# Attention sums and conformer taps on VectorE alone, and the conformer's place in w_o's order of K

## The chip, the cores and the metric

The kernel runs on one core of one Trainium2 chip. Its metric is the time of the device from start to end, in microseconds (us), the median of several executions. The core has five engines with a queue of instructions each: TensorE (PE; its weight loads are shown as PEld), VectorE (DVE), ScalarE (ACT), GpSimd (POOL) and SyncE (SP), which here only issues DMAs. An engine takes the instructions of its queue in order and waits on semaphores for what another engine or a DMA has to finish. TensorE reads its operands from SBUF and writes to PSUM.

## The reference

The reference computes two layers of a hybrid backbone over 128 context tokens and 1024 latent tokens of width 1024. In each layer three groups of heads work side by side on the projection of the normed input, and their outputs are joined and projected by `w_o`:

```python
attn_out = _blocked_attention(q, keys, vals)
conv_out = _conformer_conv(zc, p)
hy_out = _hyena(zh, p)
mix = jnp.concatenate([attn_out, conv_out, hy_out], axis=-1) @ p['w_o']
x = x + g1 * mix
```

Attention is softmax(q k / 8) v for 8 heads of 64, with 2 heads of keys and values, over 1152 keys for the latent tokens. The conformer gates its 256 channels, convolves each with 31 taps over the positions, norms them by groups and multiplies them by a 256 x 256 matrix. A convolutional feed-forward of width 2816 with a gate follows each layer. All is computed in float32; products that need it are split into a high and a low part, three matmuls in place of one.

## The kernel before

The planner that orders the queues takes the instructions of the program with a priority each, the place at which the program issued them; `high_priority(offset)` moves a stretch of them by so many places forward, a negative offset moves them back. Each engine's queue is then fixed.

A layer runs in four phases. Phase 1 norms the input, projects it and runs Hyena. Phase 2 (`phase2`) is attention, with the prompt's own attention, the conformer (`tapped_conv`) and parts of the modulation (`mod`) as generators in the background. Phase 3 (`phase3`) is the product with `w_o`, phase 4 the feed-forward.

In `attention`, j runs over 4 pairs of heads, half over 2 halves of 512 queries, c over 9 chunks of 128 keys: 72 chunks a layer. For a chunk TensorE makes the scores S^T of two heads in one PSUM tile (`st`, 128 x 1024, one buffer), ScalarE their exponentials `p` (128 x 1024 in SBUF, five buffers), and TensorE multiplies these by the values (`av`) two chunks later (`drain(2)`). The maxima that softmax needs are found ahead: `maxes(j + 1)` runs beside pair j, three products `S` and three reductions `mx` on VectorE a step, and its result goes into the score product as two more rows of q. The denominators are sums over the keys. `gather` first adds the exponentials of several chunks into a tile `es` of 128 x 1024; `finish` then multiplies each such tile by ones (`avs`, L1440) and divides. Of the nine chunks of a half, 0 and 1 are held and become the first terms of two sums; the even chunks are added on GpSimd (four adds), the odd ones on VectorE (three adds). Only in the last half of the layer does chunk 8 go into the ones product as a third part of its own, and there the reciprocals are spread by TensorE (`rs`, `orr`) and not by DMA.

`taps` convolves two blocks of 128 channels by 31 taps, with even and odd positions kept apart so that three sets of 16, 15 and 16 taps over 584 positions do it. Each tap is one VectorE instruction (L227, `ca<-cu,cws,ca`, `ca<-cd,cwh,ca`, `ca<-cu,cwh,ca`), 300 places back (`TAPS_PRIO`). Ten of the last 16 are done elsewhere: ScalarE multiplies (`cz<-cu,cwh`), GpSimd adds them up (`cz<-cz`), and one VectorE add joins them. After each VectorE tap the generator yields; `tapped_conv` hands control back every sixth time (`P2_TAPS`), and attention turns each background generator once a chunk, three times from chunk 41 on. When the taps are through, `conv` does the conformer's norms and its product, and `mix_out` writes its two blocks of output (chunks 4 and 5 of the 1024 rows of K in `w_o`) to DRAM as high and low part.

`phase3` loads the eight chunks of K, high (`mh`) and low (`ml`), each into a pool of its own; chunks 0 to 3 are attention's pairs, 4 and 5 the conformer's, 6 and 7 Hyena's. The loads are issued on SP in the order in which `w_o`'s product takes them (`MIX`), and the pools are opened in nearly the same order. The rows of `w_o` are put in that order on the host.

Of the kernel before, what the change touches and what calls it, by code (L numbers as in the profile page):

```python
# [31 lines left out]
RESIDUES = [0, 4, 2, 6, 1, 5, 3, 7]  # L32
PAIRS = [(0, 4), (2, 6), (1, 3), (5, 7)]

MIX = [6, 7, 4, 5, 0, 1, 2, 3]

# [80 lines left out]
SEGF = [(0, 386, 0, 386), (386, 770, 386, 770), (770, 1154, 770, 1152)]  # L119


P2_TAPS, TAPS_PRIO = 6, 300

SIDE_TAPS = 10

OUT_PRIO = 100

# [9 lines left out]
class Kern:  # L137
# [1236 lines left out]

    def attention(self, l, bgs):
        nc, ap, K1, K2, V = self.nc, self.ap, self.K1, self.K2, self.V
        pend, acc, fins, part, held = [], {}, [], [], {}

        def gather(j, half, c, P):

            k = c % 2
            if c < 2:
                held[k] = P
            elif j == 3 and half == 1 and c == 8:
                part.append(P)
            else:
                if c < 4:
                    part.append(ap.tile([128, 1024], F32, tag=f"e{k}", name="es", bufs=1))
                self.add(part[k][:], held[k][:] if c < 4 else part[k][:], P[:], None if k else nc.gpsimd)

        def drain(n):
            while len(pend) > n:
                j, half, c, P = pend.pop(0)
                g = j // 2
                if c == 0:
                    acc[0] = [self.sq.tile([128, 512], F32, tag=f"av{u}", name=n) for u, n in enumerate(("av", "avs"))]
                o, sm = acc[0]
                for u in range(2):
                    self.mm(o[64 * u : 64 * u + 64, :], V[:, 2 * c + g, :], P[:, 512 * u : 512 * u + 512], c == 0, c == 8)
                if c == 8:  # L1400
                    fins.append(self.finish(l, j, half, acc[0], list(part), j == 3 and half == 1))
                    part.clear()

        Q = self.first
        for j in range(4):
            g = j // 2
            cur, mg, nxt = Q, self.maxes(j + 1) if j < 3 else iter(()), None
            for half in range(2):
                for c in range(9):
                    S = self.sq.tile([128, 2, 512], F32, tag="st", name="st")  # L1410
                    for k, (K, n) in enumerate(((K1[g], 128), (K2[g], 66))):
                        for u in range(2):
                            self.mm(S[:, u, :], K[:n, 128 * c : 128 * c + 128], cur[u][k][:n, 512 * half : 512 * half + 512], k == 0, k == 1)
                    P = ap.tile([128, 1024], F32, tag="p", name="p", bufs=5)
                    self.act(P[:], S[:].rearrange("p a b -> p (a b)"), AF.Exp)
                    nxt = next(mg, nxt)
                    pend.append((j, half, c, P))
                    gather(j, half, c, P)
                    drain(2)
                    for f in fins:  # L1420
                        next(f, None)
                    for b in bgs:
                        for _ in range(3 if 9 * half + c + 18 * j > 40 else 1):
                            next(b, None)
            Q = nxt
            for Q in mg:
                pass
        drain(0)
        for f in fins:
            for _ in f:  # L1430
                pass
# [35 lines left out]
    def taps(self, l, tp):  # L1467


        nc, v, w = self.nc, self.vec[l], self.cwh[l]  # L1470

        n = 584
        for c in range(2):
            U = tp.tile([128, 1198], F32, tag="cu", name="cu", bufs=1)
            for p, q in ((0, 15), (143, 158), (1182, 1198)):
                nc.gpsimd.memset(U[:, p:q], 0.0)
            nc.sync.dma_start(U[:, 15:143], self.uD[c, :, 0:128])
            nc.sync.dma_start(U[:, 158:1182], self.uD[c, :, 128:NT])
            e, d = U[:].rearrange("p (m u) -> p u m", u=2)[:, 0, :], U[:].rearrange("p (m u) -> p u m", u=2)[:, 1, :]
            D = tp.tile([128, 598], F32, tag="cd2", name="cd2", bufs=1)  # L1480
            O = tp.tile([128, 1168], F32, tag="ca", name="ca", bufs=1)
            y0, y1 = O[:].rearrange("p (m u) -> p u m", u=2)[:, 0, :], O[:].rearrange("p (m u) -> p u m", u=2)[:, 1, :]
            h = w[:, 31 * c : 31 * c + 31]

            def low():
                return self.tc.high_priority(offset=-TAPS_PRIO)

            with low():
                self.sub(D[:], e[:, 1:599], d[:, 0:598])
                self.sub(e[:, 0:599], e[:, 0:599], d[:, 0:599])  # L1490
            yield

            Z = None
            for k in range(16 - SIDE_TAPS, 16):
                y = tp.tile([128, n], F32, tag="cz" if Z is None else "cy", name="cz", bufs=1 if Z is None else 2)
                self.act(y[:], e[:, k : k + n], AF.Copy, scale=h[:, 2 * k : 2 * k + 1])
                if Z is None:
                    Z = y
                else:
                    self.add(Z[:], Z[:], y[:], nc.gpsimd)  # L1500
            for k in range(16):
                with low():
                    s = h[:, 30:31] if k == 15 else self.cws[l][:, 15 * c + k : 15 * c + k + 1]
                    if k == 0:
                        nc.vector.tensor_scalar(y0, d[:, 0:n], s, v[:, V_CB + c : V_CB + c + 1], op0=ALU.mult, op1=ALU.add)
                    else:
                        self.stt(y0, d[:, k : k + n], s, y0, ALU.mult, ALU.add)
                yield
            for k in range(15):
                with low():  # L1510
                    self.stt(y1, D[:, k : k + n], h[:, 2 * k + 1 : 2 * k + 2], y1 if k else y0, ALU.mult, ALU.add)
                yield
            for k in range(16 - SIDE_TAPS):
                with low():
                    self.stt(y0, e[:, k : k + n], h[:, 2 * k : 2 * k + 1], y0, ALU.mult, ALU.add)
                yield
            if Z is not None:
                self.add(y0, y0, Z[:])
            nc.sync.dma_start(self.cD[c, :, 0:128], O[:, 0:128])
            nc.sync.dma_start(self.cD[c, :, 128:NT], O[:, 143:1167])  # L1520
        yield
# [56 lines left out]
    def phase3(self, l, bgf):  # L1578
# [5 lines left out]
        with ExitStack() as ctx:  # L1584
            self.use(self.ring(ctx, f"o{l}", 3, 5))
            src = self.i["xT"] if l == 0 else self.xD
            mh, ml = {}, {}
            for c in (3, 6, 7, 4, 5, 0, 1, 2):
                mp = self.pool(ctx, f"mix{l}{c}", 1, "right")
                mh[c], ml[c] = (mp.tile([128, NT], F32R, tag=t, name=t) for t in ("mh", "ml"))  # L1590
            for n, c in enumerate((6, 7, 4, 5, 0, 1, 2, 3)):
                nc.sync.dma_start(mh[c][:].bitcast(F32), self.mixD[l][0, c])
                nc.sync.dma_start(ml[c][:].bitcast(F32), self.mixD[l][1, c])
            for c in range(8):
# [289 lines left out]
```

## Time and profile before

| what | value |
|---|---|
| median of 3 runs | 3346.62 us (3346.41 to 3347.53) |
| the profiled execution's own time | 3345.59 us |
| its span, first to last instruction | 3343.3 us |
| mean granted clock of TensorE | 0.958 |
| TensorE busy | 3134.0 us, 94% |
| VectorE busy | 2160.7 us, 65% |
| ScalarE busy | 1195.1 us, 36% |
| GpSimd busy | 495.1 us, 15% |

Busy is the time in which an engine had at least one instruction running. The clock is the share of TensorE's full speed that was granted. Line numbers such as L227 are those of the kernel; many operations go through helpers and so share a line, and are told apart by their tiles, written out<-in. "pd", "up", "dn" and "wo" are phases 3 and 4, where TensorE is nearly always busy.

### The profile page before, as it was taken

Reading aid. Unit: us, or ns where it says so; the run is one execution under the profiler, and the core shown is the slowest. Engines: PE = TensorE matmul, PEld = TensorE weight load, DVE = VectorE, ACT = ScalarE, POOL = GpSimd, SP = SyncE. Lnnn points to the kernel's source line nnn. Section 1 sums busy time; section 2 is a strip of 40 time slices with the busy share of each in tenths; the row PEclk is TensorE's granted clock in tenths of the full one; section 3 lists DMA queues with packets and bytes.
Section 4 is the critical chain, followed back from the end, with each engine's and each line's share of the span. In section 5 each row is a group of like instructions: output and inputs, shape, how many; then the busy total and the mean of one; then the engine's idle time right before and its main releaser. Section 6 shows DMA issues by size and latency. Waiting matters only on the chain. (4 is left out here: it accounts for less than half of the span.)

```text
span 3343.3 us, 44669 instructions
## 1 busy us (share of the span) xinstructions
PE 3134.0 (94%) x17330; PEld 2769.0 (83%) x17330; DVE 2160.7 (65%) x3464; ACT 1195.1 (36%) x1976; POOL 495.1 (15%) x412
## 2 busy tenths in 40 slices
PE   5899778999799999999998997899999999999997
PEld 3899733449799999999998995345799999999997
DVE  6887889665765554545567896987365454554556
ACT  3433333452352222333344333435343233333223
POOL 5402234221310000000012113422110000000002
PEclk8899879999899999999999997899999999999998
DMA  7565544445311111111113446351511111111112
GB/s 280 172 224 173 158 151 168 156 161 163 127 38 42 42 44 43 42 42 44 42 56 134 161 142 212 100 164 61 190 29 51 42 42 43 43 42 42 42 44 70
DMA packets 152327, 336.08 MB, mean 101 GB/s; under 512 B 21360, under 2 KB 57844, under 8 KB 145589
## 3 DMA queue, kind: packets, MB, share of 16 engines
q1 hardware_dynamic: 147412, 318.69, 29.8%
q0 software_dynamic: 4704, 14.55, 1.5%
q8 instruction: 137, 2.24, 0.3%
q14 instruction: 74, 0.60, 0.1%
HBM read 264.86 MB, written 68.31 MB: 100 GB/s over the span
## 5 line engine op out<-in xcount | busy, mean ns | idle before, releaser
L241 PE MATMUL up<-hl,whi 128*128 128x384 f32 (+1 forms) x2112 | 712.8, 338 | 4.4 <-DVE hl L227 2.9
L241 PE MATMUL up<-hh,whi 128*128 128x384 f32 (+1 forms) x2112 | 710.3, 338 | 3.6 <-ACT hh L212 2.7
L241 PE MATMUL up<-hh,wlo 128*128 128x384 f32 (+1 forms) x2112 | 711.9, 337 | 0.0
L215 DVE TENSOR_TENSOR wlo<-wraw,whi 128x512 fp32r<-128x512 f32 x362 | 255.6, 706 | 646.6 <-ACT whi L235 646.3
L235 ACT CAST whi<-wraw 128x512 fp32r<-128x512 f32 x362 | 223.7, 618 | 848.2 <-PE dn L241 358.1
L241 PEld LDWEIGHTS up<-hl,whi 128*128 128x128 f32 x2112 | 398.7, 189 | 6.4 <-DVE hl L227 4.3
L241 PEld LDWEIGHTS up<-hh,whi 128*128 128x128 f32 x2112 | 398.7, 189 | 4.3 <-ACT hh L212 3.1
L241 PEld LDWEIGHTS up<-hh,wlo 128*128 128x128 f32 x2112 | 398.8, 189 | 0.0
L227 DVE SCALAR_TENSOR_TENSOR xt<-dn,mod,xt 128x128 f32<-128x128 f32 (+2 forms) x704 | 332.5, 514 | 71.3 <-PE dn L241 71.1
L241 PE MATMUL dn<-gh,wlo 128*128 128x384 f32 (+1 forms) x1056 | 359.0, 340 | 0.0
L241 PE MATMUL dn<-gh,whi 128*128 128x384 f32 (+1 forms) x1056 | 358.1, 339 | 0.0
L241 PE MATMUL dn<-gl,whi 128*128 128x384 f32 (+1 forms) x1056 | 357.4, 338 | 0.0
L227 DVE SCALAR_TENSOR_TENSOR fu<-pd,vec,fu 128x1154 f32<-128x1154 f32 (+2 forms) x192 | 254.0, 1324 | 91.7 <-ACT fu L212 89.2
L215 POOL TENSOR_TENSOR acc<-acc,sq 128x384 f32<-128x384 f32 x51 | 55.0, 1087 | 1633.2 <-ACT sq L212 1632.2
L241 PE MATMUL win<-hl,whi 128*128 128x384 f32 x768 | 265.0, 345 | 9.5 <-DVE hl L227 5.5
L241 PE MATMUL win<-hh,whi 128*128 128x384 f32 x768 | 264.0, 347 | 3.4 <-ACT hh L235 1.1
L241 PE MATMUL win<-hh,wlo 128*128 128x384 f32 x768 | 263.8, 344 | 0.0
L1357 DVE TENSOR_REDUCE mx<-S 128x1 f32<-128x384 f32 x384 | 196.6, 548 | 37.4 <-PE S L241 36.5
L1678 ACT COPY pd<-up 128x384 f32<-128x384 f32 (+1 forms) x352 | 131.8, 401 | 239.1 <-PE up L241 239.1
L212 ACT ACTIVATE p<-st 128x1024 f32<-128x1024 f32 x144 | 147.1, 1022 | 158.3 <-PE st L241 157.9
L241 PEld LDWEIGHTS dn<-gl,whi 128*128 128x128 f32 x1056 | 199.9, 189 | 0.0
L241 PEld LDWEIGHTS dn<-gh,whi 128*128 128x128 f32 x1056 | 199.7, 189 | 0.0
(294 smaller groups left out, 5196.7 us busy)
## 6 DMA issues: line engine op xcount, KB each, us to landing
wmod<-in_w_mod SPq DMA_DIRECT2D x48, 1024.0 KB
wraw<-in_w_up SPq DMA_DIRECT2D x176, 256.0 KB
wraw<-in_w_dn SPq DMA_DIRECT2D x88, 256.0 KB
wraw<-in_w_in SPq DMA_DIRECT2D x64, 256.0 KB
q<-qD SPq DMA_DIRECT2D x48, 256.0 KB
mh<-mixD SPq DMA_DIRECT2D x16, 576.0 KB
ml<-mixD SPq DMA_DIRECT2D x16, 576.0 KB
khD<-fK SPq DMA_DIRECT2D x16, 512.0 KB
```

The costliest lines, as they stand in the source:

```text
L212: return self.nc.scalar.activation(out, in_, f, **k)
L215: return (eng or self.nc.vector).tensor_tensor(out, a, b, op=op)
L227: return (eng or self.nc.vector).scalar_tensor_tensor(out, a, s, b, op0=op0, op1=op1)
L235: self.nc.scalar.copy(hi, src)
L241: self.nc.tensor.matmul(out, l, r, start=start, stop=stop)
L1357: nc.vector.tensor_reduce(m3[:, k, s : s + 1], S[:, :384], op=ALU.max, axis=AX.X)
L1678: self.nc.scalar.copy(p[:, u + o : v + o], t[:, u - a : v - a])
```

## The change

Four edits. In `gather` the exponentials of chunks 0 to 7 are added up in one tile `e` with two buffers, seven adds on VectorE, and chunk 8 goes into the ones product as the second part, in every half. In `taps` the side sum on ScalarE and GpSimd is gone and all 47 taps a block run on VectorE; control goes back every eighth tap, and the taps stand 200 places back. The conformer's chunks 4 and 5 move in `MIX` from third and fourth to sixth and seventh, just ahead of chunk 3; the loads and the pools follow.

```diff
-MIX = [6, 7, 4, 5, 0, 1, 2, 3]
+MIX = [6, 7, 0, 1, 2, 4, 5, 3]
...
-P2_TAPS, TAPS_PRIO = 6, 300
-
-SIDE_TAPS = 10
+P2_TAPS, TAPS_PRIO = 8, 200
...
-        pend, acc, fins, part, held = [], {}, [], [], {}
+        pend, acc, fins, parts, held = [], {}, [], [], {}
...
-            k = c % 2
-            if c < 2:
-                held[k] = P
-            elif j == 3 and half == 1 and c == 8:
+            if c == 0:
+                held[0] = P
+                parts.append([])
+                return
+            part = parts[-1]
+            if c == 8:
                 part.append(P)
             else:
-                if c < 4:
-                    part.append(ap.tile([128, 1024], F32, tag=f"e{k}", name="es", bufs=1))
-                self.add(part[k][:], held[k][:] if c < 4 else part[k][:], P[:], None if k else nc.gpsimd)
+                if c == 1:
+                    part.append(ap.tile([128, 1024], F32, tag="e", name="es", bufs=2))
+                self.add(part[0][:], held[0][:] if c < 2 else part[0][:], P[:])
...
-                    fins.append(self.finish(l, j, half, acc[0], list(part), j == 3 and half == 1))
-                    part.clear()
+                    fins.append(self.finish(l, j, half, acc[0], parts.pop(0), j == 3 and half == 1))
...
-            Z = None
-            for k in range(16 - SIDE_TAPS, 16):
-                y = tp.tile([128, n], F32, tag="cz" if Z is None else "cy", name="cz", bufs=1 if Z is None else 2)
-                self.act(y[:], e[:, k : k + n], AF.Copy, scale=h[:, 2 * k : 2 * k + 1])
-                if Z is None:
-                    Z = y
-                else:
-                    self.add(Z[:], Z[:], y[:], nc.gpsimd)
...
-            for k in range(16 - SIDE_TAPS):
+            for k in range(16):
                 with low():
                     self.stt(y0, e[:, k : k + n], h[:, 2 * k : 2 * k + 1], y0, ALU.mult, ALU.add)
                 yield
-            if Z is not None:
-                self.add(y0, y0, Z[:])
...
-            for c in (3, 6, 7, 4, 5, 0, 1, 2):
+            for c in (3, 6, 7, 0, 1, 2, 4, 5):
...
-            for n, c in enumerate((6, 7, 4, 5, 0, 1, 2, 3)):
+            for n, c in enumerate(MIX):
```

## Rows read from the trace of the kernel before

**Rows 1.** The chain that ended last, layer 1: start us, us, what.

```profile
2179.94 2.71 DVE ml L215
...
2183.85 0.74 DVE ca L227
...
2186.39 1.13 DVE es L215
...
2189.35 2.23 DVE ca L227
```

**Rows 2.** From:to, us, PE PEld DVE ACT POOL busy (instructions), clock, DMA share, GB/s.

```profile
434.00:590.00 156.00, 130.26 (x527) 58.12 (x529) 148.06 (x234) 60.48 (x86) 66.11 (x34) 0.84 0.40 142
590.00:720.00 130.00, 124.75 (x632) 64.26 (x632) 91.08 (x179) 63.66 (x88) 34.77 (x15) 0.99 0.41 137
2073.00:2230.00 157.00, 132.39 (x550) 59.48 (x551) 155.65 (x236) 63.62 (x90) 66.07 (x35) 0.90 0.41 140
2230.00:2345.00 115.00, 111.06 (x540) 59.04 (x538) 86.50 (x168) 60.59 (x86) 31.25 (x13) 1.00 0.30 90
```

**Rows 3.** The same stretches, instructions that touch tile p alone; ACT counts exponentials.

```profile
434.00:590.00 156.00, 35.15 (x118) 6.32 (x120) 14.13 (x9) 30.67 (x30) 33.50 (x13) 0.84 0.40 142
590.00:720.00 130.00, 35.57 (x132) 6.41 (x132) 14.65 (x12) 33.03 (x33) 34.77 (x15) 0.99 0.41 137
2073.00:2230.00 157.00, 37.35 (x130) 6.77 (x132) 12.15 (x10) 33.77 (x34) 34.88 (x14) 0.90 0.41 140
2230.00:2345.00 115.00, 31.65 (x120) 5.87 (x118) 13.39 (x11) 30.03 (x30) 31.25 (x13) 1.00 0.30 90
```

**Rows 4.** VectorE's groups, 434 to 590 us: xcount | busy us, mean ns.

```profile
L1357 DVE TENSOR_REDUCE mx<-S 128x1 f32<-128x384 f32 x85 | 43.6, 547 | 4.5 <-PE S L241 4.4
L227 DVE SCALAR_TENSOR_TENSOR ca<-cu,cws,ca 128x584 f32<-128x584 f32 x28 | 33.3, 1189 | 0.1
L227 DVE SCALAR_TENSOR_TENSOR ca<-cd,cwh,ca 128x584 f32<-128x584 f32 x30 | 25.7, 855 | 0.0
L227 DVE SCALAR_TENSOR_TENSOR ca<-cu,cwh,ca 128x584 f32<-128x584 f32 x14 | 20.3, 1447 | 0.0
L215 DVE TENSOR_TENSOR es<-es,p 128x1024 f32<-128x1024 f32 x6 | 9.3, 1548 | 0.0
L215 DVE TENSOR_TENSOR es<-p 128x1024 f32<-128x1024 f32 x3 | 4.8, 1614 | 0.0
...
L215 DVE TENSOR_TENSOR cu<-cu 128x599 f32<-128x599 f32 x2 | 1.6, 776 | 0.0
```

**Rows 5.** VectorE's groups, 2073 to 2230 us.

```profile
L227 DVE SCALAR_TENSOR_TENSOR ca<-cu,cws,ca 128x584 f32<-128x584 f32 x28 | 37.9, 1354 | 0.1
L227 DVE SCALAR_TENSOR_TENSOR ca<-cd,cwh,ca 128x584 f32<-128x584 f32 x30 | 34.4, 1147 | 0.1
L227 DVE SCALAR_TENSOR_TENSOR ca<-cu,cwh,ca 128x584 f32<-128x584 f32 x14 | 13.5, 965 | 0.0
L215 DVE TENSOR_TENSOR es<-es,p 128x1024 f32<-128x1024 f32 x6 | 7.3, 1216 | 0.0
...
L215 DVE TENSOR_TENSOR cu<-cu 128x599 f32<-128x599 f32 x2 | 3.7, 1854 | 0.0
```

**Rows 6.** Timeline, layer 0: start us, us, engine, line, operation, tiles.

```profile
474.09 2.38 POOL L215 TENSOR_TENSOR es<-es,p 128x1024 f32<-128x1024 f32 x1 [3.90 <-ACT p L212]
474.13 2.96 DVE L227 SCALAR_TENSOR_TENSOR ca<-cu,cwh,ca 128x584 f32<-128x584 f32 x1
```

**Rows 7.** The chain that ended last, end of layer 1's attention.

```profile
2370.74 0.88 PE avs L241 x4
...
2373.34 3.77 PE wo L241 x21
```

**Rows 8.** SP's queue, timeline, layer 1: the conformer's first load for w_o.

```profile
2345.20 0.42 SPq L1592 DMA_DIRECT2D mh<-mixD  x1
```

**Rows 9.** Busy time by stretch, start of layer 0's w_o product.

```profile
748.70:754.00 5.30, 5.30 (x24) 5.30 (x25) 0.21 (x1) 0.00 (x0) 0.00 (x0) 0.68 0.99 364
```

## The prediction

> **What bounds the kernel now.** I read the page first: TensorE is busy 94% of the span and at full clock nearly everywhere, except in two stretches of slices, each around the start of an attention phase. Only these can be worth much to this change, so the second view was the busy time by stretch. Attention of a layer falls into two parts there [rows 2]. In part 1, while the conformer's taps run (434 to 590 us in layer 0, 2073 to 2230 in layer 1), VectorE is busy 148.1 of 156 us and 155.7 of 157, while TensorE is busy 130.3 and 132.4, at a clock of 0.84 and 0.90. In part 2, after the last tap, TensorE is busy 124.8 of 130 and 111.1 of 115 at a clock of 0.99 and 1.00, and VectorE 91.1 and 86.5. So VectorE sets the pace of part 1 and TensorE that of part 2. The chain that ended last says the same: in part 1 of layer 1 it goes from one VectorE instruction to the next, taps (ca), sums (es) and maxima, with hardly a TensorE piece [rows 1].
>
> The third reading is how far attention gets. A layer has 72 chunks, and one exponential (p) stands for one of them. In part 1 30 and 34 exponentials ran, in part 2 33 and 30 [rows 3]. Part 2 therefore costs 130/33 = 3.9 and 115/30 = 3.8 us a chunk.
>
> The fourth is what a VectorE instruction costs when GpSimd is at work. In the chain a free tap takes 0.74 us and a free sum 1.13; beside them stand a tap of 2.23 and an ml of 2.71 [rows 1]. One tap lasts 2.96 us, and it lies over a GpSimd sum that began 0.04 us earlier and lasted 2.38 [rows 6]. The maxima, which read PSUM, keep their 547 ns [rows 4]. So the two engines do not work side by side here: a VectorE instruction with two inputs in SBUF waits out GpSimd's. The Trainium skill, "SBUF — State Buffer", section "Who interferes with whom", has VectorE and GpSimd share one read and write port pair that is held for a whole instruction, and lets a reduction go free; by that rule, the trace agrees. The rule would also allow more than the rows show, and that is weighed at the third rival.
>
> **The taps.** Before, 72 taps a layer with a running sum ran on VectorE in 33.3 + 25.7 + 20.3 = 79.3 us [rows 4] and 37.9 + 34.4 + 13.5 = 85.8 us [rows 5]. These are durations; an instruction's start overlaps the end of the one ahead by about 0.08 us (a free es lasts 1.216 [rows 5] and holds the chain for 1.13 [rows 1]). Without it: 73.5 and 80.0 us. After, 92 such taps at the free 0.74 take 68.1 us. That is -5.4 and -11.9 us, although 20 more are on VectorE. The two adds of the side sum go, about a tap each: -1.5 a layer. ScalarE's 20 products and GpSimd's 18 adds of them go too; both engines have room, so by themselves that is nothing.
>
> **The sums of exponentials.** Before, VectorE adds 3 of the 9 chunks of a half, GpSimd 4. After, VectorE adds 7, GpSimd none, and the ninth goes straight into the ones product. In part 1 of layer 0 nine VectorE sums took 9.3 + 4.8 us [rows 4], 13.4 without the overlap. Thirty chunks are three halves of 7 sums and 2 more: 23 x 1.13 = 26.0, so +12.6. In layer 1 ten free sums, 11.3 us, become 27 for 34 chunks, 30.5: +19.2. The ones product of a half has two parts before and two after, so TensorE's work stays. The ninth exponential now holds its buffer until the product, one of five for about two chunks; as an exponential comes every 3.8 us or later, I cost that at nothing. If it were not covered, ScalarE would wait for a product that TensorE runs two chunks later anyway.
>
> **Other VectorE instructions freed.** The in-place difference cu takes 1.85 us a piece in layer 1 [rows 5] and 0.78 in layer 0 [rows 4]: -2.1. Small groups lose such waits too (ml above). Between none and some four waits of 2 us a layer, I take two: -4.0 each. VectorE's balance in part 1, for the same chunks: layer 0 -5.4 - 1.5 + 12.6 - 4.0 = +1.7, layer 1 -11.9 - 1.5 + 19.2 - 2.1 - 4.0 = -0.3. Together +1.4 us: the freed waits pay for the moved work and little else.
>
> **Where the taps end.** The queues are filled in the planner's order, so what matters next is at which chunk the last tap stands. Taps that go where VectorE has room, at the old 76 steps to 30 chunks, would with 94 steps end at chunk 37, 7 later. The offset of 200 in place of 300 pulls them forward by 100 places; a chunk's step issues some 30 to 40 instructions (4 scores, exponential, 3 products and 3 maxima, sum, 2 value products, taps and background), so that is 3 chunks. The 8 taps per turn in place of 6 keep the number of turns: (96+1)/8 = 12 against (76+1)/6 = 13. Net: 4 chunks later. A chunk more in part 1 costs VectorE there (148.1 - 73.5 + 12.6 - 4.0)/30 = 2.8 us, in layer 1 (155.7 - 80.0 + 19.2 - 6.1)/34 = 2.6, and spares part 2 between that much and its whole 3.9. I take the middle: -0.6 a chunk, 4 chunks, two layers: -4.8. The ends are 4 chunks earlier (+4.8) and 10 later (-12).
>
> **Ends of the phases.** The last half had three parts in its ones product; one goes, and it is in the chain just ahead of the phase's end: 0.88 us in layer 1 [rows 7], -1.8 for both. The conformer's place in the order of K is worth nothing by itself: the first of its loads is issued at 2345.2 [rows 8], and the first w_o product runs at 2373.3 [rows 7], 28 us later. On SP's queue 20 loads change places; before, the loads of chunks 0 to 2 and all behind them stood behind a wait for the conformer, after only chunk 3 and the loads of x do. In layer 0 these loads come in a burst, and the first w_o products run at a clock of 0.68 for 5.3 us [rows 9]; spread loads may save between 0 and 5.3 x 0.32 = 1.7 us of it. I take -0.8.
>
> **Sum.** +1.4 - 4.8 - 1.8 - 0.8 = -6.0 us. The profiled execution took 3345.59 us, 2.3 more than its span and 1.0 less than the median of 3346.62; the difference is put on the median: 3340.6 us.
>
> **Rivals.** First: the taps end earlier, because the offset decides and not VectorE's room. Then part 1 is shorter but part 2 gets more chunks: +4.8 in place of -4.8, 3350 us. For it: the offset alone moves every tap 3 chunks forward. Against: before, the last tap stood at chunk 30, long after turn 13.
>
> Second, the other side: VectorE becomes the bound of part 2. Its sums grow there by 4 in 9 chunks, 63 x 4/9 x 1.13 = 32 us over both layers, on 177.6 busy of 245 [rows 2, 3]. That makes 86%; it decides where a stretch of 20 us passes 95%, since the maxima then come late and the score products behind them in TensorE's queue stand. If half of the 32 us comes to the end, and the reach brings nothing, the time is 3346.6 + 16 + 1.4 - 1.8 = 3362. For it: part 2 has conformer work on VectorE that comes in bunches. Against: GpSimd's waits go there too.
>
> Third: a larger gain. TensorE stands idle 25.7 and 24.6 us in the two parts 1 [rows 2]. If free VectorE instructions let the maxima come when the planner's order wants them, half of that is regained: 3346.6 - 25 = 3322. For it: the waits are longest just ahead of maxima. Against: VectorE's balance is about zero. Of GpSimd's 66.1 us in each part 1 [rows 2] the taps' rows show 20 and 27 us as VectorE's loss (73.5 and 80.0 less 72 x 0.74). By the Trainium skill's rule named above all 66 could be lost, and a gain of this size would then be near.
>
> Fourth: nothing changes. VectorE's balance is zero and the last tap stands where it stood: 3346.
>
> **How the numbers follow.** About 0.2% (6.7 us) is what a measurement of this kernel can tell from no change. Forecast 0.43 (3332 to 3346; its middle lies near the bound, so 0.22 of it faster, 0.21 same), first rival 0.12 (0.06 same, 0.06 slower), second 0.13 (slower), third 0.21 (faster), fourth 0.11 (same). Faster 0.43, same 0.38, slower 0.19. The range reaches the third rival's middle below and stops short of the second's above: 3321 to 3359.
>
> **What would show it.** Right: no GpSimd sums in either attention phase, taps at 0.82 us throughout, VectorE's busy share in part 1 unchanged near 97%, 34 and 38 exponentials by the last tap, two parts in the last ones product. Wrong: exponentials by the last tap at or under 30 (first rival); TensorE in part 2 well under 95% with waits for maxima (second); TensorE over 92% in part 1 (third). Most open is the place of the last tap, which no row of before shows.

## The result, and the profile after

The changed kernel takes 3370.6 us (median; 3368.3 to 3379.6), the kernel before, run beside it, 3347.1 us. The ratio is 1.0082, 95% interval 1.0066 to 1.0098: slower by 23.5 us between these medians and by 22 to 33 us by the interval, where the forecast was 6 us faster, and outside the range.

The profiled execution is the slowest of its four, 3379.6 us, 9 above the median; that matters further down. First the stretches that answer to [rows 2]: attention up to the last tap and after it, in both layers, and in the middle the start of layer 0's w_o. Columns: from:to, us, busy us (instructions) of PE, PEld, DVE, ACT and POOL, granted clock, DMA share, GB/s.

```profile
434.00:611.00 177.00, 149.37 (x617) 66.52 (x617) 167.98 (x303) 55.18 (x79) 0.20 (x3) 0.87 0.42 142
611.00:740.00 129.00, 127.38 (x625) 63.21 (x626) 86.90 (x164) 63.05 (x86) 1.05 (x1) 0.98 0.35 123
748.00:765.00 17.00, 3.23 (x15) 2.83 (x12) 2.60 (x5) 0.62 (x1) 0.00 (x0) 0.50 1.02 392
2084.00:2270.00 186.00, 157.93 (x615) 69.32 (x614) 169.50 (x302) 55.21 (x78) 0.20 (x3) 0.84 0.42 136
2270.00:2395.00 125.00, 122.07 (x568) 63.02 (x566) 86.00 (x157) 65.66 (x91) 0.00 (x0) 0.97 0.22 75
```

GpSimd is gone from attention (0.2 us, where it was 66 in each first part). VectorE still paces part 1 and TensorE still paces part 2, 127.4 of 129 us and 122.1 of 125. The odd row is the third: for 17 us TensorE does 3.2 us of work, at a clock of 0.50, the lower of its two levels, while the DMA engines are full. Nothing like it stands in the kernel before, where w_o started at a clock of 0.68 for 5 us but without a pause [rows 9].

The same stretches for tile p alone, as in [rows 3]; ACT counts exponentials and DVE sums.

```profile
434.00:611.00 177.00, 44.70 (x160) 8.64 (x160) 34.25 (x28) 37.34 (x37) 0.87 0.42 142
611.00:740.00 129.00, 44.97 (x158) 8.73 (x160) 34.20 (x28) 36.30 (x36) 0.98 0.35 123
2084.00:2270.00 186.00, 46.58 (x160) 8.88 (x160) 34.17 (x28) 37.88 (x37) 0.84 0.42 136
2270.00:2395.00 125.00, 45.07 (x160) 8.73 (x160) 34.22 (x28) 35.77 (x35) 0.97 0.22 75
```

Thirty-seven exponentials run in each first part, against 30 and 34. VectorE's groups in layer 0's first part answer to [rows 4]: count | busy us, mean ns of one | idle before.

```profile
L213 DVE TENSOR_TENSOR es<-es,p 128x1024 f32<-128x1024 f32 x24 | 29.4, 1224 | 0.0
L225 DVE SCALAR_TENSOR_TENSOR ca<-cu,cwh,ca 128x584 f32<-128x584 f32 x34 | 28.2, 830 | 0.0
L225 DVE SCALAR_TENSOR_TENSOR ca<-cd,cwh,ca 128x584 f32<-128x584 f32 x30 | 25.0, 833 | 0.0
L225 DVE SCALAR_TENSOR_TENSOR ca<-cu,cws,ca 128x584 f32<-128x584 f32 x28 | 23.0, 820 | 0.1
L213 DVE TENSOR_TENSOR es<-p 128x1024 f32<-128x1024 f32 x4 | 4.9, 1217 | 0.1
```

All taps are at their free length, 820 to 833 ns. So the arithmetic on VectorE went as forecast, and the loss is elsewhere. The chain that ended last shows it at the end of layer 0's attention: start us, us, what.

```profile
740.66 1.46 PE pw L239 x6
...
742.15 0.59 ACT cvo L210
...
742.76 0.52 ACT mh L233
...
743.30 8.86 DMA mixD<-mh
...
753.50 8.71 DMA mh<-mixD
...
762.26 2.93 PE wo L239 x8
```

The conformer's output (pw, cvo, mh) is on the path. Before, in layer 1, the first load for w_o behind its writes was issued 28 us ahead of the first w_o product [rows 7, 8], and the chain ran from the last ones product (avs) to wo. Here the output comes after the last exponential and takes 8.9 us to memory, and a load for w_o behind it takes another 8.7. SP's queue shows what stands ahead of each: start us, us, engine, line, operation, tiles, count.

```profile
737.11 4.16 SPq L1583 DMA_DIRECT2D xt<-in_xT  x8
...
743.30 0.34 SPq L1046 DMA_DIRECT2D mixD<-mh  x1
...
746.90 3.32 SPq L1046 DMA_DIRECT2D mixD<-mh  x2
...
752.17 0.32 SPq L1580 DMA_DIRECT2D mh<-mixD  x1
...
753.50 0.42 SPq L1580 DMA_DIRECT2D mh<-mixD  x1
```

The eight loads of x (128x1152 floats each, 4.7 MB together) leave at 737.11, at the start of the last exponential. The conformer's last writes leave behind them.

Which chunk a load brings is read from the queue as the program builds it. The load at 752.17 is that of chunk 4, a conformer's; it waits for the write of 743.30, which landed at 743.30 + 8.86 = 752.16. The load at 753.50 is that of chunk 6, Hyena's, with which w_o begins (`MIX`). Its data had long been in memory. The load stood behind the conformer's writes and chunk 4's load in SP's queue, and its tiles lie in the room of the conformer's `cxh` and `cxl`, so it also had to wait for the last pw products, which end at 744.1. So a late conformer holds up the start of w_o, wherever its own chunks stand in K. By the same reading the load of [rows 8] is Hyena's chunk 7, the first one behind the conformer's last writes, and not one of the conformer's; the lead of 28 us is the same.

### The profile page after: what moved, and what is told of

It reads as the page before. It is cut to its first block, busy times and chain, and to the rows that moved or that the text cites. A ratio compares the mean times of both kernels' runs of the same rounds, so it can differ in the third digit from the quotient of the medians.

```text
span 3377.8 us, 44577 instructions
## 1 busy us (share of the span) xinstructions
PE 3146.1 (93%) x17322; PEld 2773.8 (82%) x17322; DVE 2179.2 (65%) x3564; ACT 1162.5 (34%) x1936; POOL 276.7 (8%) x314
## 4 chain that ended last, share of the span: by engine, by line
PE 81%; DVE 9%; DMA 6%; issue 2%; ACT 2%; SPq 0%; POOL 0%; DVEq 0%; ACTq 0%; POOLq 0%
PE up L239 32%; PE dn L239 16%; PE win L239 10%; PE wo L239 5%; PE av L239 4%; PE st L239 3%; PE S L239 2%; DVE ca L225 2%; DVE mx L1355 1%; PE modp L239 1%; DVE nt L225 1%; PE fc L239 1%; DVE hl L225 1%; DMA q<-qD 1%; PE flt L239 1%
## 5 line engine op out<-in xcount | busy, mean ns | idle before, releaser
L239 PEld LDWEIGHTS S<-k,q 128*128 128x128 f32 x384 | 76.9, 222 | 155.6 <-DVE mx L1355 63.4
```

Of the source, the lines that this page charges most:

```text
L239: self.nc.tensor.matmul(out, l, r, start=start, stop=stop)
```

## The experiments

For each kernel one profiled execution gave the starts of a few instructions. From them a table, in us, layer 0 / layer 1: attention from the first to the last exponential; how far the conformer's last output (cvo) starts after the last exponential (negative: ahead of it); and from the last exponential to the first product of the feed-forward (up), which holds the gap before w_o and w_o itself. Ratio is time to the kernel before on the same chip, whose median lay between 3343.2 and 3347.1 us from run to run; a loss given below in us is taken from the median of the kernel before beside it.

| kernel | attention | cvo after last exponential | to first up | time | ratio (95%) |
|---|---|---|---|---|---|
| before | 298.1 / 293.9 | -20.9 / -25.8 | 169.7 / 111.9 | 3347.1 | 1 |
| after | 296.0 / 306.2 | +7.4 / -0.6 | 188.3 / 120.8 | 3370.6 | 1.0082 (1.0066 to 1.0098) |
| e1 sums alone | 298.2 / 300.6 | -23.2 / -17.9 | 166.5 / 112.1 | 3349.5 | 1.0009 (0.9996 to 1.0023) |
| e2 taps alone | 309.7 / 301.3 | -7.6 / -7.9 | 173.8 / 116.9 | 3368.5 | 1.0077 (1.0062 to 1.0092) |
| e3 order of K alone | 299.8 / 295.4 | -17.5 / -20.8 | 168.5 / 112.4 | 3352.8 | 1.0029 (1.0017 to 1.0041) |
| e4 all but the order | 296.5 / 293.8 | +7.9 / -0.6 | 185.5 / 128.3 | 3377.7 | 1.0103 (1.0087 to 1.0118) |
| e5 before, conformer late | 293.9 / 296.2 | +9.5 / +3.4 | 185.4 / 126.5 | 3374.7 | 1.0090 (1.0073 to 1.0107) |
| e6 after, two buffers | 298.6 / 307.4 | -32.5 / -33.3 | 166.4 / 111.0 | 3353.1 | 1.0022 (1.0013 to 1.0031) |
| e7 after, ten taps fewer | 292.0 / 278.9 | -5.2 / -9.7 | 177.1 / 116.5 | 3337.0 | 0.9973 (0.9963 to 0.9984) |
| e8 sums, two buffers | 302.6 / 311.2 | -32.4 / -27.5 | 166.7 / 117.6 | 3373.3 | 1.0081 (1.0066 to 1.0096) |
| e9 before, two buffers | 314.8 / 318.4 | -35.5 / -35.9 | 168.5 / 112.3 | 3390.9 | 1.0131 (1.0105 to 1.0157) |
| e10 after, two of cu, ca | 304.5 / 301.9 | -26.2 / -38.2 | 166.4 / 111.0 | 3353.6 | 1.0030 (1.0019 to 1.0040) |
| e11 the same, old order | 302.4 / 304.6 | -27.3 / -31.8 | 166.4 / 111.1 | 3365.4 | 1.0052 (1.0037 to 1.0067) |
| e12 after, x loaded later | 291.3 / 294.1 | +7.4 / -2.9 | 179.7 / 116.1 | 3353.9 | 1.0033 (1.0020 to 1.0045) |
| e13 e12, two of cu, cd2 | 298.6 / 296.7 | -14.5 / -2.9 | 169.6 / 117.8 | 3354.5 | 1.0029 (1.0016 to 1.0041) |
| e14 before, x loaded later | 294.3 / 294.9 | -20.9 / -25.7 | 170.8 / 111.9 | 3345.4 | 1.0002 (0.9991 to 1.0014) |

Read the third and fourth columns against each other. In layer 0, wherever the conformer's last output starts 14 us or more ahead, the stretch to the feed-forward is 166 to 171 us; at 5 to 8 us ahead it is 174 to 177, and at 7 to 10 us behind 180 to 188. In layer 1 it is 111 or 112 where the output is 17 us or more ahead (e8, at 117.6, doesn't fit), 116 to 118 at 3 to 10 us ahead, and 121 to 128 where it comes with the last exponential or after it.

### The three parts alone

e1 puts the new `gather`, `drain` and `parts` into the kernel before:

```diff
...
-                self.add(part[k][:], held[k][:] if c < 4 else part[k][:], P[:], None if k else nc.gpsimd)
+                self.add(part[0][:], held[0][:] if c < 2 else part[0][:], P[:])
...
```

> The kernel before with the first edit alone: chunks 0 to 7 of a half summed on VectorE, chunk 8 into the ones product; side taps, pacing and order of K as before. Theory (reach): the loss of the whole change comes from the last tap standing later, so that the conformer's chain ends after attention and w_o waits for its loads. With 37 taps a block on VectorE as before, the conformer's last output stays some 20 us ahead of the end of attention, and the time is 3342 to 3350 us. Rival (VectorE's work): the 32 more sums a layer are the cost by themselves; then attention of a layer lasts 5 to 10 us longer and the time is 3357 us or more.

It made no measurable difference, 3349.5 us. In its layer 0, first part, VectorE runs 23 sums where it ran nine, in 148.1 us of busy time as before (434 to 593 us, 31 exponentials), because the taps beside them are freer than in [rows 4]: 1049, 823 and 825 ns against 1189, 855 and 1447.

```profile
L227 DVE SCALAR_TENSOR_TENSOR ca<-cu,cws,ca 128x584 f32<-128x584 f32 x28 | 29.4, 1049 | 0.1
L227 DVE SCALAR_TENSOR_TENSOR ca<-cd,cwh,ca 128x584 f32<-128x584 f32 x29 | 23.9, 823 | 0.0
L215 DVE TENSOR_TENSOR es<-es,p 128x1024 f32<-128x1024 f32 x19 | 23.2, 1220 | 0.3 <-ACT p L212 0.3
L227 DVE SCALAR_TENSOR_TENSOR ca<-cu,cwh,ca 128x584 f32<-128x584 f32 x14 | 11.5, 825 | 0.0
L215 DVE TENSOR_TENSOR es<-p 128x1024 f32<-128x1024 f32 x4 | 4.9, 1222 | 0.5 <-ACT p L212 0.5
```

e2 has the tap edit alone (side sum out, 16 taps in the last loop, 8 and 200):

```diff
...
-            for k in range(16 - SIDE_TAPS):
+            for k in range(16):
...
```

> The kernel before with the second edit alone: all 47 taps of a block on VectorE, control back every eighth tap, offset 200; sums split between VectorE and GpSimd as before, order of K as before. Theory (reach): the last tap stands later, but less than in the whole change, as VectorE has fewer sums between its taps; the conformer ends about 10 us ahead of the end of attention, and the time is 3345 to 3355 us. Rival (VectorE's work): 20 taps more at 0.74 us on an engine that paces part 1 cost some 15 us a layer less the waits for the side sum's GpSimd adds, 3355 to 3365 us with the conformer still in time.

3368.5 us: nearly the whole loss, and above both ranges that were expected. Its conformer is 7.6 and 7.9 us ahead, too little, but the stretches behind attention give only 9 us (4.1 and 5.0). The larger part is attention, 11.6 and 7.4 us longer than before, with GpSimd's sums still beside the taps. So the loss of this edit by itself is for the most part not lateness.

e3 has the order of K and of the pools alone, and e4 everything but that:

```diff
-MIX = [6, 7, 4, 5, 0, 1, 2, 3]
+MIX = [6, 7, 0, 1, 2, 4, 5, 3]
...
```

> The kernel before with the third edit alone: order of K 6, 7, 0, 1, 2, 4, 5, 3, loads and pools with it. Theory (reach): the order does not matter while the conformer ends in time: 3344 to 3351 us. Rival (order): the loads of w_o's first chunks now lie in room that the conformer gives back, or stand behind it on SP's queue, and w_o starts 5 to 15 us later in each layer after its last output: 3357 to 3375 us.

> The changed kernel with the old order of K, loads and pools. Theory (reach): the conformer ends as late as in the changed kernel, and now w_o takes its chunks third and fourth, so the time is that of the changed kernel or more, 3368 to 3380 us. Rival (order): 3344 to 3352 us.

The order alone costs 0.29%, between the two ranges that were expected; no stage of its profile stands out, and where that comes from stays open. With the other two parts the order makes no difference that the intervals separate (1.0082 and 1.0103). In layer 1, where the conformer is just late, the changed kernel's w_o stretch is 120.8 us against 128.3 with the old order, as a later place for these chunks should give; in layer 0 it is 188.3 against 185.5, the other way.

### Is it the late conformer?

e5 takes the kernel before, with its taps, sums and order, and only delays the second block's result: 16 copies on ScalarE before it is written.

```diff
+            for _ in range(16 * c):
+                self.act(O[:, 0:1167], O[:, 0:1167], AF.Copy)
             nc.sync.dma_start(self.cD[c, :, 0:128], O[:, 0:128])
```

> The kernel before with 16 copies of the second block's sum onto itself on ScalarE, about 1.3 us each, between its last tap and its write to DRAM. VectorE, GpSimd and TensorE have the same work; only the conformer starts some 20 us later, so that its last output stands at the last exponential of a layer, as in the changed kernel. Theory (lateness): the loss of the changed kernel is that of the late conformer, and this kernel shows most of it, 3360 to 3375 us. Rival (VectorE's work on the way, lateness only a part): w_o starts some 4 us later in each layer, 3349 to 3358 us.

3374.7 us. Lateness alone gives as much loss as the change. Attention is as long as before (293.9 and 296.2 us), and the stretch behind it grows by 15.7 and 14.6 us, 30.3 together, where the medians differ by 29.0. In the 22 us behind the last exponential TensorE is busy for 11.4, and in SP's queue the conformer's writes again leave behind the loads of x, and the first load for w_o, chunk 6's as the queue is built, behind them:

```profile
740.00:762.00 22.00, 11.37 (x66) 7.37 (x63) 6.67 (x13) 7.54 (x14) 0.00 (x0) 0.72 0.95 341
```

```profile
739.68 4.04 SPq L1597 DMA_DIRECT2D xt<-in_xT  x8
748.00 0.33 SPq L1048 DMA_DIRECT2D mixD<-mh  x1
...
757.00 0.40 SPq L1594 DMA_DIRECT2D mh<-mixD  x1
```

e6 and e7 take the lateness away from the changed kernel in two ways. In e6 cu, cd2 and ca have two buffers, so that the second block's taps needn't wait for the first's:

```diff
-            U = tp.tile([128, 1198], F32, tag="cu", name="cu", bufs=1)
+            U = tp.tile([128, 1198], F32, tag="cu", name="cu", bufs=2)
```

> The changed kernel with two buffers in place of one for the taps' tiles (cu, cd2, ca), so that the second block of taps need not wait until the first is written out and its input loaded. VectorE's work is that of the changed kernel; the last tap stands some 14 chunks earlier in its queue and the conformer's last output at chunk 59 or 60 of 72. Theory (lateness): 3340 to 3352 us. Rival (VectorE's work): part 1 is paced by it as before, 3360 to 3370 us.

e7 leaves ten taps of each block out and so does less work:

```diff
-            for k in range(16):
+            for k in range(6):
```

> The changed kernel without ten of the 47 taps of a block, those which ran on ScalarE and GpSimd before; they are left out altogether. VectorE has 15 us a layer less to do, and the conformer's last output stands at chunk 69 and 67 of 72 in place of 72 and 71. Theory (lateness): most of the loss goes, 3345 to 3355 us. Rival (the sums on VectorE are the cost once the taps are there too): 3358 us or more.

e6 is at 3353.1 us with both w_o stretches short, 166.4 and 111.0 us: the loss is 7.4 us where it was 23.5. But attention in layer 1 is 13.5 us longer than before. e7, with 16.4 us less of taps a layer (20 x 0.82), is at 3337.0 us, faster than the kernel before by 0.27% and below the range expected for it, with its conformer only 5 and 10 us ahead. So the load on VectorE has a price too, apart from lateness.

### The same early taps beside GpSimd

e8 is the kernel before with the sums edit and two buffers, e9 with the two buffers alone.

> The kernel before with the sums on VectorE (the first edit alone) and two buffers for the taps' tiles: the side sum stays on ScalarE and GpSimd, the conformer ends at chunk 59 to 61. Theory (lateness): without the sums' kernel's late conformer in layer 1 it loses nothing, and what VectorE no longer waits for GpSimd may show: 3336 to 3347 us. Rival (part 1 is paced by VectorE, and earlier taps only crowd it): 3350 us or more.

> The kernel before with nothing but two buffers each for cu, cd2 and ca, so that the second block's taps need not wait for the first's; GpSimd keeps its ten taps a block and its eight sums a head. By position its last tap stands at 74 and 83 maxima of 192 (104 and 109 before) and the conformer's last output at exponential 58 of 72. It tells what made the sums edit with two buffers slow (3373). Theory A: taps crowded into the front part are what costs, there GpSimd's additions stand beside more of VectorE's taps and stretch them; then this kernel, with GpSimd's sums beside them too, is slower than before as well, 3360 to 3385. Theory B: it is the sums edit together with the early taps (24 more additions on VectorE in the crowded part); then this kernel is near before, 3340 to 3355. In both the gap between the last exponential and w_o's first product is near 6 us.

Both have their conformer 27 us or more ahead, and both are slow: 3373.3 and 3390.9 us. This was not what I had thought of e8; e9 was run for it, and came out slow as its first theory said, 6 us above that theory's range. The cost is in attention, 314.8 and 318.4 us in e9. VectorE's taps and GpSimd's work there, layer 0, up to the last tap:

```profile
L227 DVE SCALAR_TENSOR_TENSOR ca<-cu,cws,ca 128x584 f32<-128x584 f32 x28 | 33.8, 1219 | 0.1
L227 DVE SCALAR_TENSOR_TENSOR ca<-cd,cwh,ca 128x584 f32<-128x584 f32 x30 | 33.4, 1121 | 0.0
L227 DVE SCALAR_TENSOR_TENSOR ca<-cu,cwh,ca 128x584 f32<-128x584 f32 x14 | 14.3, 1020 | 0.0
...
L215 POOL TENSOR_TENSOR cz<-cz 128x584 f32<-128x584 f32 x18 | 33.6, 1864 | 57.8 <-ACT cz L212 56.9
L215 POOL TENSOR_TENSOR es<-es,p 128x1024 f32<-128x1024 f32 x6 | 15.5, 2576 | 19.1 <-ACT p L212 19.1
```

And in e6, where GpSimd has none of this, in the same part:

```profile
L225 DVE SCALAR_TENSOR_TENSOR ca<-cu,cwh,ca 128x584 f32<-128x584 f32 x33 | 27.2, 827 | 0.0
L225 DVE SCALAR_TENSOR_TENSOR ca<-cd,cwh,ca 128x584 f32<-128x584 f32 x30 | 24.8, 828 | 0.0
L225 DVE SCALAR_TENSOR_TENSOR ca<-cu,cws,ca 128x584 f32<-128x584 f32 x28 | 23.3, 844 | 0.1
```

Ninety-one taps take 75.3 us there, 72 take 81.5 in e9. But slower taps are not what makes e9 dearer than the kernel before, whose 72 took 79.3 and 85.8 us [rows 4, 5]; in e9's layer 1 they took 76.6. What differs is where they stand. When the last tap starts, 18 and 19 chunks are through in e9, where it was 30 and 32, and from the first exponential to there TensorE is idle 34.5 and 35.3 us, against 22.3 and 24.6 in the kernel before. It is so in the other kernels with early taps too: 35.4 and 37.9 us in e8, and 29.6 and 35.0 in e6, where GpSimd has no work beside the taps. Where the taps stand early, the sums edit is worth some 18 us (loss of 45.7 in e9, 27.6 in e8) and the tap edit, here with the new order of K, another 20 (7.4 in e6). How much of these 18 and 20 is GpSimd's additions is not shown.

### Taps between early and late

e10 doubles cu and ca alone, e11 does that with the old order of K.

> The changed kernel with two buffers for cu and ca alone (cd2 keeps one). By position the last tap stands at 93 and 96 maxima of 192 (126 in the changed kernel, 81 and less with all three doubled), the conformer's last output at exponential 62 and 57 of 72. Lateness theory: the conformer is in time, the gap before w_o 5 to 7 us in both layers, and the attention of the second layer loses less than with three doubled, since the taps are spread over more of it: 3335 to 3350, the best of the kernels with all the taps. Load theory (VectorE's whole load decides, wherever it stands): as with three buffers, 3353 within 4. If early taps alone were no help: near the changed kernel, 3365 to 3375.

> The last one with the order of K of before (the conformer's chunks 4 and 5 third and fourth in w_o). The conformer is in time here, so its products need no place near the end; the order alone on the kernel before cost 0.29%. If the order costs by itself: 5 to 10 us below the one with the new order, 3330 to 3345. If its place matters only where the conformer is late: the same within 3 us.

Both have the conformer in time, and neither beats e6: 3353.6 and 3365.4 us. For e10 the lateness theory expected 3335 to 3350 and missed; the load theory, 3353 within 4, came out. The spread of e11's runs is wide (3352.8 to 3370.4), and its profiled execution has the same stages as e10's, so I take from it only that the old order is not better.

### What makes lateness dear

e12 is the changed kernel with the loads of x put behind w_o's own: each x tile first gets one column, copied from the conformer's last chunk as loaded.

```diff
             for c in range(8):
+                self.act(x[c][:, 0:1], mh[5][:, 0:1].bitcast(F32), AF.Copy)
                 nc.sync.dma_start(x[c][:], src[:, c])
```

> The changed kernel, but the eight loads of x (4.7 MB a layer) are made to come after w_o's own loads: each x tile first gets one column from ScalarE, copied from the conformer's last chunk as loaded for w_o. Taps, sums and the order of K are those of the changed kernel; by position the conformer's last output still stands behind the last exponential in layer 0 (72 of 72) and at 70 of 72 in layer 1. In the changed kernel layer 0's last write of the conformer's took 8.9 us and the first load for w_o 8.7 us, behind the x loads. Theory A (the late conformer costs what its data need in a DMA queue that the x loads have filled): the gap between the last exponential and w_o's first product falls in layer 0 from 25.1 to 12 to 18 us, and the time to 3352 to 3365. Theory B (the conformer's lateness alone decides, the x loads don't matter): gap 22 to 27 us in layer 0, time 3366 to 3378.

3353.9 us: with the conformer as late as in the changed kernel (+7.4 us), the loss is 10.2 us where it was 23.5, and the stretches behind attention are 13.3 us shorter (8.6 and 4.7). The chain after the last exponential of layer 0, to set beside the changed kernel's:

```profile
738.68 0.59 ACT cvo L210
739.30 0.52 ACT mh L233
739.84 1.88 DMA mixD<-mh
741.73 3.92 DMA mh<-mixD
```

The load of 741.73 is that of chunk 4. The load of chunk 6 and the product that waits for it:

```profile
743.57 0.39 SPq L1580 DMA_DIRECT2D mh<-mixD  x1
...
749.14 1.33 PE L239 MATMUL wo<-mh,whi 128*128 128x384 f32 x3 [3.55 <-DMA mh<-mixD]
```

The write takes 1.88 us, not 8.86, so chunk 4's load and those behind it leave SP sooner; w_o's first product starts 5.6 us after the issue of chunk 6's load, not 8.8. x's loads now leave SP at 765. The gap from the last exponential to the first w_o product is 15.5 us, not 25.1.

Two runs asked what the rest is, and whether the loads' order is worth something anyway. e13 is e12 with two buffers for cu and cd2; e14 is the kernel before with e12's edit.

> The changed kernel with the loads of x behind w_o's own (as in the run before) and two buffers each for cu and cd2. By position the taps still end late (114 and 126 maxima of 192, 126 and 129 in the run before), but layer 0's last conformer output stands at exponential 65 of 72 instead of 72, layer 1's at 70 as before. In the run before the gap ahead of w_o was 15.5 us in layer 0 and 7.0 in layer 1, against 5 to 7 in kernels whose conformer is in time; attention took 291 and 294 us. If lateness is all that is left of the changed kernel's loss: layer 0's gap 5 to 8 us, the time 8 to 10 us below the run before, 3341 to 3348, level with the kernel before or a little faster. If VectorE's load costs the rest: attention in layer 0 some 7 us longer than 291 and the time 3350 to 3356.

> The kernel before with nothing but the loads of x behind w_o's own. Its conformer is in time (gap 6.8 and 5.9 us). If the order of the loads is worth something by itself, also where the conformer is in time, the gaps fall by 1 to 2 us each and w_o's start runs without a stall: 3338 to 3344. If it matters only behind a late conformer: 3343 to 3350, no measurable difference. If the copies and the later x cost: over 3352, with a wait of w_o's first sum for x.

e14 makes no measurable difference: the order of the loads matters only behind a late conformer. e13 stayed at 3354.5 us, though layer 0's gap is down to 8.3 us, so lateness in layer 0 is not what was left. What was expected if VectorE's load costs the rest came out: 3350 to 3356 us, with attention in layer 0 some 7 us longer than e12's 291 (298.6). Its layer 1 is still somewhat late: from the last exponential to the first up it takes 117.8 us, against 111.9 before. The busy time of that stretch, in the kernel before and then in e13:

```profile
2367.30:2479.20 111.90, 108.81 (x639) 104.96 (x635) 42.48 (x80) 28.21 (x52) 1.27 (x7) 1.00 0.33 110
```

```profile
2368.00:2486.00 118.00, 112.45 (x637) 107.75 (x635) 42.02 (x79) 28.16 (x58) 1.33 (x7) 0.97 0.41 143
```

TensorE is idle 5.6 us instead of 3.1, and the same products take 3.6 us more at a mean clock of 0.97 instead of 1.00. Of the other 5 us, attention shows 3.3 (0.5 and 2.8) against the kernel before. Differences of this size, and the 7 us against e12, are small beside e13's own runs, which spread over 15.7 us (3346.8 to 3362.5), and each is read from one execution.

No kernel that does all the work was faster than the one before.

## Why the prediction was wrong

**What bounds the kernel** was read rightly for attention. The views stopped, though, at the first w_o product, as if what comes after attention could only wait for attention.

**Taps, sums, freed waits.** Right. The 92 taps took 76.2 us in layer 0 and, less the overlap of 0.08 each, 68.8 against a forecast of 68.1. Part 1 hardly changed its pace: from the first exponential to the start of the last tap it took 168.3/36 = 4.7 us a chunk in layer 0, where it had taken 143.2/30 = 4.8, and 5.1 in layer 1, where it had taken 4.8. Over both attentions VectorE's busy time rose by 18 us (484.9 to 502.8, in 308 and 303 us from each first exponential), less than the forecast's +1.4 in part 1 and the second rival's 32 in part 2 make together.

**Where the taps end.** The direction was right, by a wrong sum. 37 chunks by the last tap were forecast from VectorE's room, less 3 for the offset. In layer 0 the trace shows 36 when the last tap starts. The offset does nothing: the changed kernel built with 300, 200, 0 and -400 has every engine's instructions in the same order. So the forecast's 4 chunks more were 6 in layer 0 (30 to 36), and 4 in layer 1 (32 to 36).

**The price of a later chunk is the step that failed.** I took a later end of the taps as pure gain, -0.6 us a chunk, and in layer 0 it is one for attention itself: layer 0's attention is 2.1 us shorter than before in the changed kernel and 6.8 in e12, whose taps end as late (layer 1 shows no gain, 294.1 us in e12 against 293.9). But the conformer stands behind the last tap. From the last tap to its last output is a chain of 115 to 135 us (588 to 722 and 2227 to 2341 us before, 609 to 744 and 2266 to 2390 after). Counted from each layer's first exponential, the last tap starts 25 and 28 us later and the last output 26 and 38; the cover was 20.9 and 25.8 us, measured to the last exponential. I had that cover in hand, as the 28 us between the conformer's first load and the first w_o product [rows 7, 8], and used it only to price the order of K at nothing, "worth nothing by itself". It should have been subtracted from the move of the taps. The forecast's own 4 chunks at 4.8 us are 19 us, which leaves 2 us of the cover in layer 0 and 7 in layer 1, where the table already shows losses. The price of the order was off too: e3 measured 0.29%.

How the loss adds up in the profiled execution. The stretches behind attention, in the kernel before and in the changed one:

```profile
742.80:912.50 169.70, 153.39 (x855) 140.39 (x853) 104.23 (x173) 46.96 (x84) 31.05 (x26) 0.95 0.48 159
```

```profile
737.00:925.00 188.00, 157.43 (x862) 144.31 (x861) 107.13 (x179) 50.59 (x92) 31.95 (x27) 0.91 0.50 171
2390.00:2511.00 121.00, 112.36 (x638) 107.56 (x636) 41.69 (x79) 28.23 (x52) 1.27 (x7) 0.96 0.39 142
```

In layer 0 TensorE is idle 30.6 us where it was idle 16.3, and busy 4.0 us longer at a lower clock. Taken between the instructions, the stretch behind attention grew by 188.3 - 169.7 = 18.6 us in layer 0 and 120.8 - 111.9 = 8.9 in layer 1, 27.5 in all, against 23.5 between the medians. The two profiled executions themselves differ by 34.0 us, the rest being attention (-2.1 and +12.3) and an earlier start of layer 0's (-3.6). Layer 1's 12.3 us are not in e4 and e12, which with the same taps and sums have 293.8 and 294.1 us there; this execution is 9 us above its median, and I don't build on it. e5 shows that lateness alone can cost as much as the change lost, e6 that the loss falls to 7.4 us without it, and e12 that with x's loads out of the way lateness costs some 13 us less. The Trainium skill's page "DMA: Bandwidth & Descriptors", section "Queues, rings and completion order", says that an SDMA engine takes a ring's descriptors in order; by that, a small write behind 4.7 MB of loads waits for them to be started. The trace agrees, 8.86 us against 1.88 without the loads ahead. It doesn't tell waiting in order from sharing: in e12 the loads of x are gone from the whole stretch, and the DMA engines, full in the changed kernel (a share of 1.02 from 748 to 765 us), are at 0.48 from the last exponential to the first w_o product.

**Ends of the phases.** The clock and the spread of the loads were to save 0.8 us. The loads came instead in one burst, 392 GB/s, with TensorE idle and then at the lower level. The last ones product has two parts, as said, and its gain shows where the conformer is in time: from the last exponential to the first w_o product it is 5.1 us in both layers of e6, e8, e10 and e11, and 5.9 in both of e9, which has the old sums. That is 0.8 a layer, for 0.9 forecast; in the changed kernel it is lost in the longer gap.

**The rivals.** The second had the right side, and its 3362 us is only 8.6 below the result, but by luck: TensorE stays at 98% in part 2, and VectorE is not the bound there. The first named the price of the reach with the sign that attention has, and e6, e9 and e10 bear it out: taps ending earlier make attention longer (layer 1: 307.4, 318.4 and 301.9 us). Against the kernel before, e9's taps end 12 and 13 chunks earlier and its attention is 16.7 and 24.5 us longer, 1.4 and 1.9 us a chunk, where the forecast had 0.6. None of them had the conformer's output as the late one. The third's regain didn't come: TensorE stands idle 27.6 and 28.1 us in the two first parts, no less than before.

**What stays open.** The kernels with all 92 taps on VectorE in which the conformer was brought forward or made cheaper end 7 to 11 us above the one before (e6, e10, e12, e13), and e11 20 us. e7 says that VectorE's load has a price: it ends 8.7 us below the kernel before, where the changed kernel is 23.5 above, 32 us in all, of which the stretch behind attention gives 15.5 (188.3 to 177.1 and 120.8 to 116.5), and the rest comes with 33 us less of taps. What e10 and e13 were expected to show if the load is the rest came out in both. But how much of the 7 to 11 us is load, how much early taps and how much a remainder of lateness is not separated by these runs, nor is e3's 0.29% explained.

## What to carry to other kernels

When an edit moves the end of a background stage, list what hangs on that stage, with the length of the chain behind it, and set its last output against the phase that needs it: a margin of 20 to 28 us is a term of the sum and can be used up. What hangs on a stage is more than its result: here the first load of the next phase, of other data, stood behind the late writes in SP's queue and in room that the stage gives back. What a missed margin costs depends on what is queued ahead of the late transfers: here a bulk load that nobody needed yet turned a gap of 15.5 us into 25.1, and moving it back took some 13 us off the loss. Where a background stage stands has a price of its own, so the gain of an edit has to be read where the work will stand.

## What the runs showed of the hardware

A write of 128x384 floats took 8.86 us behind eight loads of 128x1152 floats on the same queue, and 1.88 us without these ahead (e12). The load of 128x1152 floats that w_o's first product waits for took 8.71 us with the DMA engines full (a share of 1.02); in e12 that product started 5.6 us after the load's issue.

VectorE and GpSimd stretch each other: beside VectorE's taps GpSimd's add of 128x584 took 1864 ns on the mean and its sum of 128x1024 2576 in e9 (the shortest of each in that run 1412 and 2356), while the taps took 1020 to 1219 ns on the mean, and 827 to 844 with GpSimd free (e6). The Trainium skill, "SBUF — State Buffer", section "Who interferes with whom", names the shared read port as an exclusive lock, in which whoever comes second waits; the trace agrees, in both directions.

ScalarE's in-place copies of 128x1167 (e5) took 1175 ns each on the mean, and attention beside them kept its length (293.9 and 296.2 us, against 298.1 and 293.9).
